# The attention output of a decoder trunk, split into upper and lower part per two head pairs instead of per four

## The chip, the cores and the metric

The kernel runs on one core of a Trainium2 chip. The metric is the device time of one execution in microseconds (us). Five engines take part, each with an instruction stream of its own that it runs in order: TensorE (PE in the profile; its weight loads are PEld), VectorE (DVE), ScalarE (ACT), GpSimd (POOL) and SyncE (SP), which issues most loads. They wait for one another by semaphores.

## The reference

A trunk of two layers on 256 tokens with 1024 channels, in float32. The first layer mixes tokens with a recurrent block, the second with forgetting attention over 16 heads of 64 channels. Each layer has a SwiGLU FFN ahead of and behind its mixer. The part that is changed is the attention:

```python
def forgetting_attention(xq, w_q, w_o, k, v, c):
    q = (xq @ w_q).reshape(Bn, S, N_HEADS, HEAD_DIM).transpose(0, 2, 1, 3) * (HEAD_DIM ** -0.5)
    for blk in range(S // Q_BLOCK):              # two blocks of 128 queries
        q0 = blk * Q_BLOCK; end = q0 + Q_BLOCK
        logits = einsum('bhqd,bhkd->bhqk', q[:, :, q0:end], k[:, :, :end])
        logits = logits + c[:, :, q0:end, None] - c[:, :, None, :end]
        logits = where(kpos <= qpos, logits, -inf)
        p = softmax(logits, axis=-1)
        outs.append(einsum('bhqk,bhkd->bhqd', p, v[:, :, :end]))
    o = concatenate(outs, axis=2).transpose(0, 2, 1, 3).reshape(Bn, S, D_ATTN)
    return o @ w_o
```

Its result goes through an RMS norm and is added to the residual stream; then comes the last FFN.

## The kernel before

**Numbers.** TensorE gets each float32 operand as two parts: an upper part, rounded to TensorE's fp32r type, and a lower part, the difference. A product is three matmuls: `mm3` gives upper by upper (L207), upper by lower of the weights (L208), and lower by upper (L209). Every weight is loaded into a tile `raw` and split by `split`: ScalarE copies it to `whi` (L199), VectorE subtracts to get `wlo` (L200). The attention output is split in the same way, into `oh` (L1206, ScalarE) and `ol` (L1207, VectorE).

**Tokens and work items.** The 256 tokens are two halves t of 128. Work comes as items, each with one weight tile of 128x1024. For each half there are eight items of the query projection and then eight of the output projection W_o. W_o's item k (`row_items`, L474) multiplies the k-th 128 rows of W_o, which belong to one pair of heads, by tile k of `oh` and `ol`; it takes six matmuls, three for each half of the 1024 columns. The last two items of a half are done together, column half by column half.

**The attention of one half** (`attention(t)`, L1143) goes by groups of heads: half 0 sees 128 keys and has four groups of two pairs, half 1 sees 256 keys and has eight groups of one pair. Each group passes through four parts:

- logits: matmuls of keys and queries (L1162) into two of the banks 4 to 7, bias (L1169) and maximum (L1171) on VectorE, exponentials with their sums (L1177) on ScalarE, reciprocal (L1179) and multiplication (L1180) on VectorE, into a tile `pe`;
- turn: four transposes of `pe` on TensorE (L1186) into a bank, copied out by ScalarE as `pT` (L1188);
- values: matmuls of `pT` with the values (L1200) into an accumulator `po`, one 128x128 block for each pair;
- the split of `po` into `oh` and `ol` (L1206, L1207), once its 512 columns are full, so for every four pairs.

Step i of a half does the values of group i-3, the turn of group i-2 and the logits of group i, in this order.

**What sets the order.** TensorE's stream is the order of the code, and that is set by a string, `ATT_ORDER`: "0" and "1" are the next item of half 0 or 1, "a0" and "a1" the next step of the attention of half 0 or 1. It runs from `0 0 0 0 0 0 0 a0 0 a0 1 1 1 a0 1 1 a0 1 1 a0 1 a1 0 a0` over alternating `a1 0` and `a1 1` to `1 1 1 1`. The streams of VectorE and ScalarE are put in order when the program is built, by a scheduler with times of its own; some parts have priority there, the residual update (`enter`) among them.

**The banks.** The accumulators, `po`, the transposes and the query tokens share banks 0 to 3 of PSUM, one tile `pall`:

```python
    def bank(kind, hold=False, again=False):

        free = [i for i in order[kind] if i not in held and i not in lent]
        i = free[-1 if again else 0]
        order[kind].remove(i)
        order[kind].append(i)
```

`mmbank()` takes the free bank that was asked for longest ago and holds it until `release`. The turn asks with `again=True` and gets the free bank that was asked for last. A bank may be written again when all that reads its old content has run, and matmuls wait for that. While half 0 is under way, W_o's accumulators and those of the query projection hold one or two of the four banks.

**Around the change**, W_o of half 0 begins after the fifth "a0" and W_o of half 1 after W_o of half 0, whose end starts its residual update on VectorE (L312, L316). `htok` (L1026) and `qT` (L1032) are the queries' tokens and their transposed copy. `nb` is the bias, `mx`, `sm` maximum and sum, `rstd` the norm's factor.

Of the kernel before, what the change touches and what calls it, by code (L numbers as in the profile page):

```python
# [9 lines left out]
F32 = mybir.dt.float32  # L10
F32R = mybir.dt.float32r
BF16 = mybir.dt.bfloat16
AF = mybir.ActivationFunctionType
ALU = mybir.AluOpType
AX = mybir.AxisListType

P = 128
D = 1024
S = 256
# [25 lines left out]
def trunk_kernel(ctx: ExitStack, tc: tile.TileContext, A: dict, out: bass.AP):  # L45
    nc = tc.nc
# [11 lines left out]
    def nm(s):  # L58
        uid[0] += 1
        return f"{s}_{uid[0]}"  # L60
# [6 lines left out]
# [6 lines that stand above are left out]
        b = pall[:, i, :]  # L73
        if hold:
            held[i] = b
        return b

    def release(*banks):
        for b in banks:
            for i in [i for i, v in held.items() if v is b]:  # L80
                del held[i]

    def mmbank():
        return bank("mm", True)
# [1040 lines left out]
    att = {}  # L1125
# [17 lines left out]
    def attention(t):  # L1143

        ap = pools["a"]
        nk = t + 1
        per = 4 // nk
        np_ = per // 2
        w = nk * P
        box = {}  # L1150
        G = NH // per

        def head(hg, b, j):
            return 2 * (hg * np_ + j) + b

        def logits(hg):
            c = 4 + (hg % 2) * 2
            lg = pall[:, c:c + 2, :S]
            for j in range(np_):
                for b in range(2):  # L1160
                    p = hg * np_ + j
                    nc.tensor.matmul(lg[:, b, j * w:(j + 1) * w], att["q"][t][b * HD:(b + 1) * HD, p, :],  # L1162
                                     kv["kT"][b * HD:(b + 1) * HD, p, :w], start=True, stop=True)
            v = lg.rearrange("p b (j k) -> p j b k", j=np_)
            h0 = hg * per
            bias = att["nb"][t][:, h0:h0 + per, :].rearrange("p (j b) k -> p j b k", b=2)
            if np_ == 1:
                v, bias = lg, att["nb"][t][:, h0:h0 + per, :]
            nc.vector.tensor_tensor(v, v, bias, ALU.add)  # L1169
            mx = spool.tile([P, 4], F32, tag="mx", name=nm("mx"))[:, :per]  # L1170
            nc.vector.tensor_reduce(mx, lg.rearrange("p b (j k) -> p b j k", j=np_), AX.X, ALU.max, negate=True)  # L1171
            sm = spool.tile([P, 4], F32, tag="sm", name=nm("sm"))[:, :per]
            pe = box["pe", hg] = ap.tile([P, per, w], F32, tag="pe", name=nm("pe"), bufs=2)
            for b in range(2):
                for j in range(np_):
                    i = b * np_ + j
                    nc.scalar.activation(pe[:, i, :], lg[:, b, j * w:(j + 1) * w], AF.Exp, bias=mx[:, i:i + 1],  # L1177
                                         accum_out=sm[:, i:i + 1])
            nc.vector.reciprocal(sm, sm)  # L1179
            nc.vector.tensor_tensor(pe, pe, sm.unsqueeze(2).to_broadcast([P, per, w]), ALU.mult)  # L1180

        def turn(hg):
            tp = bank("mm", again=True)
            pev = box["pe", hg].rearrange("p a b -> p (a b)")
            for j in range(4):
                nc.tensor.transpose(tp[:, j * P:(j + 1) * P], pev[:, j * P:(j + 1) * P], ident)  # L1186
            pT = box["pT", hg] = ap.tile([P, 4, P], F32, tag="pT", name=nm("pT"), bufs=2)
            nc.scalar.activation(pT.rearrange("p a b -> p (a b)"), tp, AF.Copy)  # L1188

        def values(hg):  # L1190
            p0 = hg * np_
            if p0 % 4 == 0:
                box["po"] = mmbank()
            po, pT = box["po"], box["pT", hg]
            for j in range(np_):
                o = (p0 + j) % 4 * P
                for k in range(nk):
                    for b in range(2):
                        hd = head(hg, b, j)
                        nc.tensor.matmul(po[b * HD:(b + 1) * HD, o:o + P], kv["v"][k][:, hd * HD:(hd + 1) * HD],  # L1200
                                         pT[:, (b * np_ + j) * nk + k, :], start=k == 0, stop=k == nk - 1)
            if (p0 + np_) % 4 == 0:
                b = (p0 + np_) // 4 - 1
                oh_v = att["oh"][t][:, 4 * b:4 * b + 4, :].rearrange("p a b -> p (a b)")
                ol_v = att["ol"][t][:, 4 * b:4 * b + 4, :].rearrange("p a b -> p (a b)")
                nc.scalar.activation(oh_v, po, AF.Copy)  # L1206
                nc.vector.tensor_tensor(ol_v, po, oh_v.bitcast(F32), ALU.subtract)  # L1207
                release(po)

        steps = []  # L1210
        for i in range(G + 3):
            s = []
            if 0 <= i - 3 < G:
                s.append(lambda i=i: values(i - 3))
            if 0 <= i - 2 < G:
                s.append(lambda i=i: turn(i - 2))
            if i < G:
                s.append(lambda i=i: logits(i))
            steps.append(s)
        return steps  # L1220
# [13 lines left out]
    ffn_d = ffn_items(lambda: pools["f"], A["ffn2_w_gate"][1], A["ffn2_w_up"][1], A["ffn2_w_down"][1], A["ffn2_post_g"][1],  # L1234
                      lambda t, hid: None, last=True)

    ATT_ORDER = ("0 0 0 0 0 0 0 a0 0 a0 1 1 1 a0 1 1 a0 1 1 a0 1 a1 0 a0 0 a1 0 a0 0 a1 0 a1 0 a1 0 a1 0 a1 1 a1 1 a1 1 a1 1 a1 1 1 1 1")


    def half(t, i):  # L1240
# [106 lines left out]
    nxt = [n_ffn3, n_ffn3]  # L1347
    for c in ATT_ORDER.split():
        if c[0] == "a":
# [45 lines left out]
```

## Time and profile before

| | us |
|---|---|
| median of 3 runs (1004.5 to 1004.77) | 1004.73 |
| the profiled execution | 1004.95 |
| its span, first to last instruction | 1003.2 |
| TensorE busy | 985.8 |
| VectorE busy | 676.1 |
| ScalarE busy | 562.1 |
| last W_o matmul of half 1 starts at | 810.14 |
| L1206, four copies of 128x512, each | 0.60 |
| L1207, four subtractions of 128x512, each | 0.68 |

In a row of the timeline stand the start, the duration, the engine, the line, the operation with output and inputs, the size, the count, and in brackets the idle time ahead of it on its engine with what ended that. A row with xN merges N instructions that follow each other. Matmuls overlap: one of 512 columns shows some 0.39 us, though the next starts 0.23 later. In a row of stretches stand from:to, length, and for PE, PEld, DVE, ACT and POOL the busy time and count, then the granted TensorE clock (1.00 is full), the DMA share and GB/s. In a row of groups stand line, engine, operation, sizes, count, then busy us and mean ns of one.

### The profile page before, as it was taken

To read this page: it belongs to the slowest core of one execution; us is meant where nothing else is said; L and a number is where in the kernel's file an instruction comes from. 1 tells how busy PE (TensorE), PEld (TensorE's weight loads), DVE (VectorE), ACT (ScalarE), POOL (GpSimd) and SP (SyncE) were. 2 spreads that over 40 slices of the span, in tenths; PEclk is the share of its full clock that TensorE was granted. 3 is DMA by queue.
4 is the path that set the end of the run, shared out by engine and by line. 5 is a ranking of instruction groups with operands and counts; after the bars stand their busy time and mean duration, and the time that the engine had idled before them with its cause. 6 is when DMAs were issued, how large, how long until landed. Compare 5 with 4: busy or idle time off the path is not lost.

```text
span 1003.2 us, 13846 instructions
## 1 busy us (share of the span) xinstructions
PE 985.8 (98%) x5272; PEld 831.9 (83%) x5272; DVE 676.1 (67%) x784; ACT 562.1 (56%) x732; POOL 50.8 (5%) x97
## 2 busy tenths in 40 slices
PE   8999999999999999999999999999999999999997
PEld 5888888789988888888898888888876678888886
DVE  5877664668998676664596676674588757666642
ACT  5656544559986555543565455553466656555431
POOL 1500000000003000000000000000030000000000
PEclk9999999999999999999999999999999999999999
DMA  6886655565427666545468666655485157665431
GB/s 231 275 272 200 199 164 189 156 184 151 137 81 248 214 188 186 189 158 186 114 204 277 190 181 196 199 188 160 156 294 168 43 151 248 188 191 187 153 123 42
DMA packets 94104, 182.06 MB, mean 181 GB/s; under 512 B 11838, under 2 KB 33430, under 8 KB 93910
## 3 DMA queue, kind: packets, MB, share of 16 engines
q1 hardware_dynamic: 92790, 180.06, 57.5%
q10 hardware_dynamic: 608, 1.06, 0.3%
q8 instruction: 41, 0.67, 0.3%
q0 software_dynamic: 640, 0.07, 0.1%
q14 instruction: 25, 0.20, 0.1%
HBM read 180.09 MB, written 1.06 MB: 181 GB/s over the span
## 4 chain that ended last, share of the span: by engine, by line
PE 68%; issue 22%; ACT 5%; DVE 4%; POOL 1%; DMA 0%; DVEq 0%; POOLq 0%; ACTq 0%
PE pall L232 23%; PE pall L233 12%; PE pall L207 9%; PE pall L209 9%; PE pall L208 9%; PE pall L858 1%; PE pall L214 1%; PE pall L215 1%; PE pall L216 1%; ACT junk L246 1%; DVE wlo L200 1%; ACT whi L199 1%; POOL rstd L241 1%; PE pall L255 1%; DVE h L316 1%
## 5 line engine op out<-in xcount | busy, mean ns | idle before, releaser
L200 DVE TENSOR_TENSOR wlo<-raw,whi 128x1024 fp32r<-128x1024 f32 (+4 forms) x329 | 395.0, 1207 | 249.5 <-ACT whi L199 246.8
L199 ACT ACTIVATE whi<-raw 128x1024 fp32r<-128x1024 f32 (+4 forms) x329 | 342.2, 1045 | 297.8 <-PE pall L209 119.1
L232 PE MATMUL pall<-xall,whi 128*128 128x512 f32 x1216 | 427.1, 397 | 0.0
L233 PE MATMUL pall<-xall,wlo 128*128 128x256 f32 x1216 | 339.6, 279 | 0.0
L232 PEld LDWEIGHTS pall<-xall,whi 128*128 128x128 f32 x1216 | 228.3, 188 | 55.2
L233 PEld LDWEIGHTS pall<-xall,wlo 128*128 128x128 f32 x1216 | 229.1, 188 | 0.1
L207 PE MATMUL pall<-whi,hid 128*128 128x512 f32 (+2 forms) x400 | 153.1, 383 | 0.5 <-ACT v L1109 0.5
L209 PE MATMUL pall<-whi,hid 128*128 128x512 f32 (+2 forms) x400 | 152.4, 381 | 0.0
L208 PE MATMUL pall<-wlo,hid 128*128 128x512 f32 (+2 forms) x400 | 152.3, 381 | 0.0
L207 PEld LDWEIGHTS pall<-whi,hid 128*128 128x128 f32 x400 | 75.1, 188 | 14.6 <-ACT v L1109 0.8
L208 PEld LDWEIGHTS pall<-wlo,hid 128*128 128x128 f32 x400 | 75.1, 188 | 13.6
L209 PEld LDWEIGHTS pall<-whi,hid 128*128 128x128 f32 x400 | 75.1, 188 | 13.7
L207 PE MATMUL pall<-whi,xall 128*128 128x512 f32 (+2 forms) x168 | 67.1, 399 | 0.4 <-DVE t L312 0.3
L208 PE MATMUL pall<-wlo,xall 128*128 128x512 f32 (+2 forms) x168 | 64.9, 386 | 0.4 <-DVE wlo L1258 0.2
L209 PE MATMUL pall<-whi,xall 128*128 128x512 f32 (+2 forms) x168 | 64.9, 386 | 0.1
L239 POOL TENSOR_SCALAR nv<-ss 128x1 f32<-128x1 f32 x24 | 10.2, 425 | 937.0 <-ACT junk L246 936.9
L208 PEld LDWEIGHTS pall<-wlo,xall 128*128 128x128 f32 x168 | 31.7, 188 | 7.5 <-DVE wlo L200 1.2
L209 PEld LDWEIGHTS pall<-whi,xall 128*128 128x128 f32 x168 | 31.5, 188 | 7.1 <-DVE xall L269 1.2
L207 PEld LDWEIGHTS pall<-whi,xall 128*128 128x128 f32 x168 | 31.6, 188 | 6.9 <-DVE t L312 0.7
L604 ACT ACTIVATE hid<-prod 128x1024 fp32r<-128x1024 f32 (+1 forms) x21 | 20.6, 981 | 23.0 <-DVE prod L600 23.0
L310 DVE SCALAR_TENSOR_TENSOR t<-pall,rstd,gb 128x512 f32<-128x512 f32 x16 | 11.9, 749 | 26.7 <-ACT junk L246 26.7
L594 ACT ACTIVATE sil<-sil 128x1024 f32<-128x1024 f32 (+1 forms) x21 | 20.6, 982 | 14.3 <-DVE sil L593 14.2
(192 smaller groups left out, 1007.9 us busy)
## 6 DMA issues: line engine op xcount, KB each, us to landing
raw<-in_ffn_w_down_dram SPq DMA_DIRECT2D x88, 512.0 KB
raw<-in_ffn_w_up_dram SPq DMA_DIRECT2D x80, 512.0 KB
raw<-in_ffn_w_gate_dram SPq DMA_DIRECT2D x79, 512.0 KB
raw<-in_rg_w_in_dram SPq DMA_DIRECT2D x20, 504.0 KB
raw<-in_rg_w_out_dram SPq DMA_DIRECT2D x10, 504.0 KB
raw<-in_ffn_w_gate_dram SPq DMA_DIRECT2D x18, 256.0 KB
raw<-in_ffn_w_up_dram SPq DMA_DIRECT2D x16, 256.0 KB
raw<-in_w_kv_dram SPq DMA_DIRECT2D x8, 512.0 KB
```

What stands on the lines that cost most here:

```text
L199: nc.scalar.activation(hi[:parts, c:c + m], rawv[:, c:c + m], AF.Copy)
L200: nc.vector.tensor_tensor(lo[:parts, c:c + m], rawv[:, c:c + m], hi[:parts, c:c + m].bitcast(F32), ALU.subtract)
L207: nc.tensor.matmul(ps, xh, wh, start=first, stop=False)
L208: nc.tensor.matmul(ps, xh, wl, start=False, stop=False)
L209: nc.tensor.matmul(ps, xl, wh, start=False, stop=last)
L214: nc.tensor.matmul(ps, wh, xh, start=first, stop=False)
L232: nc.tensor.matmul(o, wh, both, start=k == 0, stop=False)
L233: nc.tensor.matmul(oh, wl, upper, start=False, stop=k == 7)
L239: nc.gpsimd.tensor_scalar(v, ss[:, 0:1], ss[:, 1:2] if n == 2 else 0.0, D * EPS * f * f, ALU.add, ALU.add)
L310: nc.vector.scalar_tensor_tensor(t1[n], pf[n], r_in, gb[:, n * 512:(n + 1) * 512], ALU.mult, ALU.mult)
L594: nc.scalar.activation(s, s, AF.Silu)
L604: nc.scalar.activation(hv, pv, AF.Copy)
```

## The change

`po` is split whenever two pairs are in it, not four, so it uses only the first 256 columns of its bank. In half 0 each group now takes a bank for `po`, fills it, splits it and releases it; in half 1 that takes two groups. The copies and subtractions are eight instead of four, with 256 columns each. The string `ATT_ORDER` is only broken into two lines and has the same entries.

```diff
         def values(hg):
             p0 = hg * np_
-            if p0 % 4 == 0:
+            if p0 % 2 == 0:
                 box["po"] = mmbank()
             po, pT = box["po"], box["pT", hg]
             for j in range(np_):
-                o = (p0 + j) % 4 * P
+                o = (p0 + j) % 2 * P
...
-            if (p0 + np_) % 4 == 0:
-                b = (p0 + np_) // 4 - 1
-                oh_v = att["oh"][t][:, 4 * b:4 * b + 4, :].rearrange("p a b -> p (a b)")
-                ol_v = att["ol"][t][:, 4 * b:4 * b + 4, :].rearrange("p a b -> p (a b)")
-                nc.scalar.activation(oh_v, po, AF.Copy)
-                nc.vector.tensor_tensor(ol_v, po, oh_v.bitcast(F32), ALU.subtract)
+            if (p0 + np_) % 2 == 0:
+                k0 = p0 + np_ - 2
+                oh_v = att["oh"][t][:, k0:k0 + 2, :].rearrange("p a b -> p (a b)")
+                ol_v = att["ol"][t][:, k0:k0 + 2, :].rearrange("p a b -> p (a b)")
+                nc.scalar.activation(oh_v, po[:, :S], AF.Copy)
+                nc.vector.tensor_tensor(ol_v, po[:, :S], oh_v.bitcast(F32), ALU.subtract)
                 release(po)
```

TensorE's stream keeps its 4894 rows and their order. The banks differ: before, `po` of half 0 is in bank 3 and then bank 0, and the turns of groups 1, 2 and 3 write banks 0, 2 and 2. Now `po` of the four groups is in banks 3, 0, 2 and 2, and the turns of groups 1, 2 and 3 write banks 3, 0 and 2, each right behind the values of the group before; the first turn of half 1 writes bank 2. The built program lets the first transpose of each of these four turns wait for the L1207 subtraction of the bank it writes. In half 1 `po` is always in bank 0, and its next use waits for the last L1207.

VectorE's stream differs from the values of group 0 on. Before, from the weight subtraction that runs beside these values (numbers at the end of names count buffers; `pe_6645` and `sm_6644` belong to group 2 of half 0, `pe_6696` and `sm_6695` to group 3):

```order
L200 TENSOR_TENSOR wlo_6675<-raw_6672,whi_6674 128x1024
L1179 RECIPROCAL sm_6644<-sm_6644 128x4
L1169 TENSOR_TENSOR pall<-pall,nb_6455 128x2x2x128
L1180 TENSOR_TENSOR pe_6645<-pe_6645,sm_6644 128x512
L1171 TENSOR_REDUCE mx_6693<-pall 128x4
L200 TENSOR_TENSOR wlo_6717<-raw_6714,whi_6716 128x1024
L200 TENSOR_TENSOR wlo_6729<-raw_6726,whi_6728 128x1024
L1179 RECIPROCAL sm_6695<-sm_6695 128x4
L1026 TENSOR_SCALAR htok_6750<-pall,rstd_6511 128x512
L1180 TENSOR_TENSOR pe_6696<-pe_6696,sm_6695 128x512
L1207 TENSOR_TENSOR ol_6470<-pall,oh_6468 128x512
```

The same place on VectorE now (group 3 is `pe_6698`, `sm_6697`):

```order
L200 TENSOR_TENSOR wlo_6675<-raw_6672,whi_6674 128x1024
L1179 RECIPROCAL sm_6644<-sm_6644 128x4
L1207 TENSOR_TENSOR ol_6470<-pall,oh_6468 128x256
L1180 TENSOR_TENSOR pe_6645<-pe_6645,sm_6644 128x512
L1169 TENSOR_TENSOR pall<-pall,nb_6455 128x2x2x128
L1171 TENSOR_REDUCE mx_6695<-pall 128x4
L1179 RECIPROCAL sm_6697<-sm_6697 128x4
L1180 TENSOR_TENSOR pe_6698<-pe_6698,sm_6697 128x512
L200 TENSOR_TENSOR wlo_6719<-raw_6716,whi_6718 128x1024
L200 TENSOR_TENSOR wlo_6731<-raw_6728,whi_6730 128x1024
L1207 TENSOR_TENSOR ol_6470<-pall,oh_6468 128x256
```

The first subtraction stands right behind the reciprocal of group 2; the second behind the whole softmax of group 3, which has moved ahead of the two weight subtractions.

ScalarE's stream at the same place, before (`pT_6686` is the turn of group 1, `qT` a query tile):

```order
L199 ACTIVATE whi_6674<-raw_6672 128x1024
L1188 ACTIVATE pT_6686<-pall 128x512
L1177 ACTIVATE pe_6645,sm_6644<-pall,mx_6642 128x128 x4
L199 ACTIVATE whi_6716<-raw_6714 128x1024
L1032 ACTIVATE qT_6466<-pall 128x512
L199 ACTIVATE whi_6728<-raw_6726 128x1024
L1177 ACTIVATE pe_6696,sm_6695<-pall,mx_6693 128x128 x4
L1206 ACTIVATE oh_6468<-pall 128x512
```

And ScalarE's now:

```order
L199 ACTIVATE whi_6674<-raw_6672 128x1024
L1206 ACTIVATE oh_6468<-pall 128x256
L1177 ACTIVATE pe_6645,sm_6644<-pall,mx_6642 128x128 x4
L1188 ACTIVATE pT_6688<-pall 128x512
L1177 ACTIVATE pe_6698,sm_6697<-pall,mx_6695 128x128 x4
L1032 ACTIVATE qT_6466<-pall 128x512
L199 ACTIVATE whi_6718<-raw_6716 128x1024
L199 ACTIVATE whi_6730<-raw_6728 128x1024
L1206 ACTIVATE oh_6468<-pall 128x256
```

The first copy stands ahead of the exponentials of group 2, the copy of the transposes behind them; both weight copies stand behind the exponentials of group 3. The streams of GpSimd and SyncE keep their rows and order.

More of the change, by code (lines that the diff above doesn't have):

```diff
@@ L1235, in trunk_kernel @@
                       lambda t, hid: None, last=True)
-    ATT_ORDER = ("0 0 0 0 0 0 0 a0 0 a0 1 1 1 a0 1 1 a0 1 1 a0 1 a1 0 a0 0 a1 0 a0 0 a1 0 a1 0 a1 0 a1 0 a1 1 a1 1 a1 1 a1 1 a1 1 1 1 1")
+    ATT_ORDER = ("0 0 0 0 0 0 0 a0 0 a0 1 1 1 a0 1 1 a0 1 1 a0 1 a1 0 a0 0 a1 0 a0 0 a1 0 a1 0 a1 0 a1 0 a1 "
+                 "1 a1 1 a1 1 a1 1 a1 1 1 1 1")
     def half(t, i):
```

## The prediction

> **What bounds the kernel now.** I read the page's engine table first, then the busy time by stretches (from 745 us, just ahead of the attention's first exponentials, to 815, where the last FFN has begun, and from there to 1000), then the timeline of the attention.
>
> ```profile
> PE 985.8 (98%) x5272; PEld 831.9 (83%) x5272; DVE 676.1 (67%) x784; ACT 562.1 (56%) x732; POOL 50.8 (5%) x97
> ...
> 745.00:815.00 70.00, 65.14 (x388) 45.82 (x387) 55.76 (x83) 46.21 (x113) 5.32 (x8) 1.00 0.44 138
> 815.00:1000.00 185.00, 181.75 (x939) 154.44 (x937) 106.81 (x99) 86.54 (x95) 2.74 (x7) 1.00 0.50 158
> ```
>
> TensorE is busy 98% of the span: what its in-order stream loses or wins in the attention reaches the end nearly whole. In the first stretch it misses 4.9 us of 70, VectorE is at 80%, and the DMA share of 0.44 leaves room; after 815 TensorE hardly waits, so nothing later gives a delay back. The timeline shows what the change aims at, the waits of the first W_o matmuls for the two parts of the attention output:
>
> ```profile
> 764.95 0.47 PE L207 MATMUL pall<-whi,oh 128*128 128x512 f32 x1 [0.30 <-ACT pT L1188]
> 767.18 0.66 PE L1200 MATMUL pall<-pT,v 128*64 128x128 f32 x8
> 770.81 0.50 PE L207 MATMUL pall<-whi,oh 128*128 128x512 f32 x1
> 772.39 0.66 PE L1200 MATMUL pall<-pT,v 128*64 128x128 f32 x8
> ...
> 789.19 0.50 PE L207 MATMUL pall<-whi,oh 128*128 128x512 f32 x1
> 790.88 0.68 DVE L1207 TENSOR_TENSOR ol<-pall,oh 128x512 fp32r<-128x512 f32 x1
> 791.61 0.50 PE L209 MATMUL pall<-whi,ol 128*128 128x512 f32 x1 [1.69 <-DVE ol L1207]
> 792.74 0.66 PE L1200 MATMUL pall<-pT,v 128*64 128x128 f32 x8
> ...
> 802.13 0.66 PE L1200 MATMUL pall<-pT,v 128*64 128x128 f32 x8
> 803.84 0.50 PE L207 MATMUL pall<-whi,oh 128*128 128x512 f32 x1 [1.04 <-ACT oh L1206]
> 805.25 0.50 PE L209 MATMUL pall<-whi,ol 128*128 128x512 f32 x1 [0.68 <-DVE ol L1207]
> ```
>
> **What it removes.** Undisturbed, the six matmuls of a W_o item take 772.39 - 770.81 = 1.58 us. The first item of token half 0 takes 767.18 - 764.95 = 2.23; the first of half 1, 792.74 - 789.19 = 3.55. The later start at 803.84 comes 1.71 after the values matmuls, where 0.59 is usual (756.14 to 756.73, below), and its third matmul 1.41 after the first, where 2/6 of 1.58 = 0.53 is usual. In the change the two tiles that each of these items reads are split a group or two earlier, so all go: 0.65 + 1.97 + 1.12 + 0.88 = 4.62 us. At 792.74, though, the next values matmuls now open a new accumulator in bank 0, which they may write only when the lower part of the one before has been read from it. That subtraction stays behind the two residual updates and starts at 790.88; at half width it ends near 791.28, TensorE goes on at 791.33 where it would have been ready at 789.19 + 1.58 = 790.77: 0.56 comes back. Gain: 4.06.
>
> **What it adds on the other engines.** Four more copies and four more subtractions, each of half the width. Neither width stands here, so the nearest rows are taken:
>
> ```profile
> L295 ACT ACTIVATE rrow<-pall 128x256 f32<-128x256 f32 x5 | 1.9, 379 | 5.0 <-PE pall L293 5.0
> L936 DVE TENSOR_TENSOR y<-pall,tt 126x256 f32<-126x256 f32 x2 | 0.8, 404 | 0.0
> ```
>
> 0.38 and 0.40 us. Beside TensorE's 70 us that is hidden; it counts only where TensorE waits for it.
>
> **What it adds on TensorE: a wait in front of the transposes.** TensorE's own instructions and their order stay as they are. In token half 0 a group fills two tiles, so the accumulator is now taken and released within one step, and the transposes that follow ask for the free bank taken last: that very bank. Before, the accumulator was held over two groups, and they got another one. So three turns (transposes of groups 1, 2, 3) now wait until ScalarE and VectorE have both read the bank, and where the scheduler put these reads decides:
>
> ```profile
> 756.14 0.66 PE L1200 MATMUL pall<-pT,v 128*64 128x128 f32 x8
> 756.24 1.06 ACT L199 ACTIVATE whi<-raw 128x1024 fp32r<-128x1024 f32 x1 [0.29 <-PE pall L209]
> 756.73 0.66 PE L1186 MATMUL pall<-ident,pe 128*128 128x128 f32 x4
> 757.01 2.35 DVE L200 TENSOR_TENSOR wlo<-raw,whi 128x1024 fp32r<-128x1024 f32 x2
> 757.31 0.71 PE L1162 MATMUL pall<-kT,qT 64*128 64x128 f32 x8
> 759.44 0.18 DVE L1179 RECIPROCAL sm<-sm 128x4 f32<-128x4 f32 x1
> 759.54 0.67 DVE L1169 TENSOR_TENSOR pall<-pall,nb 128x512 f32<-128x512 f32 x1
> 761.96 0.66 PE L1186 MATMUL pall<-ident,pe 128*128 128x128 f32 x4
> ...
> 779.18 0.70 DVE L1169 TENSOR_TENSOR pall<-pall,nb 128x512 f32<-128x512 f32 x1
> 780.72 0.48 ACT L1177 ACTIVATE pe<-pall,mx 128x256 f32<-128x256 f32 x1 [1.61 <-DVE mx L1171]
> ...
> 762.44 0.35 ACT L1177 ACTIVATE pe<-pall,mx 128x128 f32<-128x128 f32 x1
> 763.72 0.21 ACT L1177 ACTIVATION_READ_ACCUMULATOR pe<-pall,mx 128x1 f32 x1
> ...
> L1032 ACT ACTIVATE qT<-pall 128x512 f32<-128x512 f32 x4 | 2.4, 601 | 2.0 <-PE pall L1031 2.0
> 751.75 2.05 ACT L199 ACTIVATE whi<-raw 128x1024 fp32r<-128x1024 f32 x2
> ```
>
> *Turn 1* (756.73). The subtraction now stands on VectorE behind two weight subtractions and a reciprocal. The former end at 757.01 + 2.35 = 759.36. The reciprocal needs four exponentials, ahead of which the copy now stands: 756.24 + 1.06 + 0.38, plus 1.49 for the four (762.44 to 763.93), gives 759.17, which is earlier. Reciprocal at 759.36, subtraction 0.10 later (759.44 to 759.54), end 759.86, and 0.05 to TensorE (790.88 + 0.68 = 791.56 to 791.61): 759.91. Cost 3.2 us.
>
> *Turn 2* (761.96, of its own 4.65 after the logits matmuls of 757.31, which move with turn 1). Its subtraction stands behind the whole softmax of those logits and two weight subtractions; ScalarE reaches the weights only after four exponentials and a query copy. From the logits' start: 0.71 + 0.05; bias and maximum until the exponentials 1.54 (779.18 to 780.72); four of them 1.49; copy 0.60; first weight copy 1.06; both weight subtractions 2.35; ours 0.40; 0.05. Sum 8.25, less about 0.2, since an instruction starts some 0.1 before the one ahead of it ends (two weight copies take 2.05, not 2.12): 8.05. Cost 8.05 - 4.65 = 3.4 us.
>
> *Turn 3*: here both reads follow at once: matmuls 0.66, copy 0.38, subtraction 0.40, three handovers of 0.05, less the usual 0.59: 1.0 us.
>
> ```profile
> 774.36 0.68 DVE L1207 TENSOR_TENSOR ol<-pall,oh 128x512 fp32r<-128x512 f32 x1
> 774.47 0.60 PE L1186 MATMUL pall<-ident,pe 128*128 128x128 f32 x4
> ...
> 781.97 0.69 DVE L1180 TENSOR_TENSOR pe<-pe,sm 128x512 f32<-128x512 f32 x1
> 782.62 0.66 PE L1200 MATMUL pall<-pT,v 128*64 128x128 f32 x8
> ...
> 795.74 0.68 DVE L1180 TENSOR_TENSOR pe<-pe,sm 128x512 f32<-128x512 f32 x1
> 796.73 0.66 PE L1186 MATMUL pall<-ident,pe 128*128 128x128 f32 x4
> ```
>
> *Three small ones in half 1.* Its first turn (774.47) reuses that bank too; the subtraction, now 0.40, ends at 774.76: 0.35. The values matmuls of 782.62 wait for a subtraction that stands behind the multiplication of 781.97: 782.66 + 0.40 + 0.05, cost 0.45. The turn at 796.73 needs a multiplication that ends 0.31 before it (796.42); TensorE comes 1.41 earlier there (1.97 - 0.56), so nothing is lost if that chain moves along and 1.10 if it doesn't; part of it does (the weight copy ahead of it need not wait so long), and I take 0.45.
>
> The order on SP's and GpSimd's queues stays; the weight loads behind the delayed subtractions come later together with the matmuls that need them. I cost that at nothing: the cover is the room in the DMA share and TensorE's own delay; without it a late weight would cost about its copy and subtraction, 1.06 + 1.18.
>
> **The sum.** Costs 3.2 + 3.4 + 1.0 + 0.35 + 0.45 + 0.45 = 8.85, gain 4.06, net +4.8 us. The profiled execution took 1004.95 (span 1003.2 and 1.75 around it), 0.22 over the median of 1004.73; on the median the forecast is 1009.5.
>
> **Rivals.**
>
> *The clock falls in the new gaps* (slower still). TensorE stands idle about 3.1 us before turn 1 and 3.3 before turn 2, longer than anywhere in the trace but its end:
>
> ```profile
> 1.51 3.60 PE L151 MATMUL pall<-idle 128*128 128x512 bf16 x8 [1.51 <-DVE idle L137]
> ...
> 996.37 0.39 PE L209 MATMUL pall<-whi,hid 128*128 128x512 f32 x1
> ...
> 999.50:999.75 0.25, 0.00 (x0) 0.00 (x0) 0.25 (x1) 0.00 (x0) 0.00 (x0) 0.52 0.00 0
> ```
>
> There the last matmul ends at 996.76, and the granted clock is at 0.52 from about 999.5, after 2.75 us. By that, both gaps can bring it down. At the start, not yet warm, eight 512-column matmuls take 3.60 us, 0.45 each; 1.58 / 6 = 0.26 is usual. Were it slow for about as long as it was idle, some 3.2 us, that loses 3.2 x (1 - 0.26/0.45) = 1.35 for each gap: 1010.9 for one, 1012.2 for both. Against it: the 1.69 us wait at 791.61 left the clock at 1.00. The Trainium skill (TensorE: Matmul & The Clock Gate, Part 1: The HAM clock gate) says that the clock halves after at least one idle window of some 3.4 us that runs on its own phase; by that rule neither gap holds a whole window and the sum stays 1009.5, but the fall after 2.75 us in this trace doesn't agree with a full window of idleness.
>
> *The reads follow at once.* If VectorE were free when the upper copy ends, turns 1 and 2 would cost what turn 3 does: net 3 x 1.0 + 1.25 - 4.06 = +0.2, 1004.9, no change. For it: turn 3. Against it: VectorE runs its instructions in the built order, and in both places long ones stand ahead.
>
> *Only the gain* (faster). If the turns did not meet the accumulator's bank, costs in turns 1 to 3 and in 774.47 fall away: 0.9 - 4.06 = -3.2, 1001.5. It decides whether the subtraction ends before 756.73 and 761.96. Since the copy can't start before the matmuls that end at 756.80, that needs another bank, which the rule of the bank list speaks against.
>
> **How the numbers follow.** Forecast case 0.58, clock 0.26, reads at once 0.08, only the gain 0.04, something slower than 1012.2 (late weights) 0.04. A measurement tells this kernel from no change at about 0.2%, 2 us: faster 0.04, same 0.08, slower 0.88. The range runs from 1007.1, where VectorE gets to the subtraction one weight subtraction (1.18) earlier in both turn 1 and turn 2, to 1012.2, both clock falls.
>
> **What would show it.** In the trace of the changed kernel: the L1186 transposes of groups 1 and 2 in half 0 idle over 3 us each on the lower subtraction, group 3 about 1; the waits of W_o's third matmuls for that subtraction gone; from 756 to 771 a delay that grows to about 6.5 us and comes down to about 4.8 by 815, where it stays. A clock under 1.00 near 760 or 768 shows the first rival. I am wrong if the first transposes after the values start at their usual 0.59, or if TensorE catches up after 815.

## The result, and the profile after

| | before | after |
|---|---|---|
| median, us | 1004.93 | 1010.5 |
| lowest to highest of six executions | 1004.5 to 1008.37 | 1009.72 to 1011.86 |
| the profiled execution | 1004.95 | 1009.83 |
| its span | 1003.2 | 1008.1 |

The change makes the kernel slower: the ratio is 1.0049, with a 95% interval of 1.0038 to 1.0059. The six executions after lie in two clusters, 1009.72 to 1009.83 and 1011.16 to 1011.86; the profiled one is of the lower.

The page's engine line of the kernel after, and the stretches that answer to those of before:

```profile
PE 985.9 (98%) x5272; PEld 833.1 (83%) x5272; DVE 676.4 (67%) x788; ACT 562.1 (56%) x736; POOL 52.7 (5%) x97
...
745.00:815.00 70.00, 61.43 (x368) 43.49 (x367) 51.39 (x81) 43.75 (x113) 5.02 (x6) 0.98 0.36 115
815.00:1000.00 185.00, 184.71 (x952) 156.92 (x952) 108.57 (x102) 88.56 (x97) 3.20 (x7) 1.00 0.50 165
```

TensorE has as many instructions as before and is busy as long. In the attention it stands still 8.6 us of 70, where it was 4.9, and the granted clock of that stretch is 0.98. What TensorE waits for from 745 to 825, in the view of the waits (engine, line, what released it: us in total, times, longest):

```profile
PE pall L1186 <- DVE ol L1207: 6.5, 4, 3.0
PE pall L1200 <- DVE ol L1207: 1.3, 2, 0.6
```

The waits of W_o's third matmuls (L209) for the lower part are gone. In their place four turns (L1186) and two values matmuls (L1200) wait for the lower part's reading of a bank. The timeline gives each in its place; first four rows of before that the prediction did not show, then TensorE after:

```profile
761.37 0.66 PE L1200 MATMUL pall<-pT,v 128*64 128x128 f32 x8
767.77 0.66 PE L1186 MATMUL pall<-ident,pe 128*128 128x128 f32 x4
787.38 0.66 PE L1200 MATMUL pall<-pT,v 128*64 128x128 f32 x8
810.83 0.50 PE L207 MATMUL pall<-whi,xall 128*128 128x512 f32 x1 [0.30 <-DVE t L312]
```

```profile
755.87 0.66 PE L1200 MATMUL pall<-pT,v 128*64 128x128 f32 x8
759.54 0.73 PE L1186 MATMUL pall<-ident,pe 128*128 128x128 f32 x4 [3.01 <-DVE ol L1207]
765.70 0.66 PE L1200 MATMUL pall<-pT,v 128*64 128x128 f32 x8
768.76 0.66 PE L1186 MATMUL pall<-ident,pe 128*128 128x128 f32 x4 [2.41 <-DVE ol L1207]
773.23 0.66 PE L1200 MATMUL pall<-pT,v 128*64 128x128 f32 x8
774.83 0.66 PE L1186 MATMUL pall<-ident,pe 128*128 128x128 f32 x4 [0.94 <-DVE ol L1207]
...
781.88 0.66 PE L1186 MATMUL pall<-ident,pe 128*128 128x128 f32 x4 [0.17 <-DVE ol L1207]
...
790.59 0.66 PE L1200 MATMUL pall<-pT,v 128*64 128x128 f32 x8 [0.65 <-DVE ol L1207]
...
795.35 0.66 PE L1200 MATMUL pall<-pT,v 128*64 128x128 f32 x8
...
799.42 0.66 PE L1200 MATMUL pall<-pT,v 128*64 128x128 f32 x8 [0.61 <-DVE ol L1207]
...
803.73 0.66 PE L1186 MATMUL pall<-ident,pe 128*128 128x128 f32 x4 [0.25 <-DVE pe L1180]
...
809.13 0.66 PE L1200 MATMUL pall<-pT,v 128*64 128x128 f32 x8
...
815.74 0.50 PE L207 MATMUL pall<-whi,xall 128*128 128x512 f32 x1 [0.29 <-DVE t L312]
```

The profiled execution after is 756.14 - 755.87 = 0.27 us ahead when the changed part begins. Counted from there, the delay at each place is the start after, less the start before, plus 0.27:

| place (start before, after) | delay | added here | predicted |
|---|---|---|---|
| turn 1 (756.73, 759.54) | 3.08 | +3.08 | +3.2 |
| values of group 1 (761.37, 765.70) | 4.60 | +1.52 | 0 |
| turn 2 (761.96, 768.76) | 7.07 | +2.47 | +3.4 |
| values of group 2 (767.18, 773.23) | 6.32 | -0.75 | -0.65 |
| turn 3 (767.77, 774.83) | 7.33 | +1.01 | +1.0 |
| first turn of half 1 (774.47, 781.88) | 7.68 | +0.35 | +0.35 |
| values (782.62, 790.59) | 8.24 | +0.56 | +0.45 |
| values (787.38, 795.35; then 792.74, 799.42) | 8.24, 6.95 | -1.29 | -1.97 + 0.56 |
| turn (796.73, 803.73) | 7.27 | +0.32 | +0.45 |
| first matmul behind W_o (810.83, 815.74) | 5.18 | -2.09 | -1.12 - 0.88 |

5.18 less the 0.27 is 4.91, and the spans differ by 4.9: all of it comes from the attention. One line was not in the forecast's sum, the 1.52 us between turn 1 and the values of group 1, where TensorE waits for nothing. The view of stretches shows what it is:

```profile
759.50:760.00 0.50, 0.46 (x4) 0.42 (x4) 0.50 (x1) 0.00 (x0) 0.00 (x0) 1.00 0.73 180
760.00:760.50 0.50, 0.50 (x4) 0.30 (x4) 0.09 (x1) 0.19 (x1) 0.00 (x0) 0.50 1.03 401
...
763.00:763.50 0.50, 0.50 (x3) 0.40 (x2) 0.00 (x0) 0.46 (x3) 0.00 (x0) 0.58 0.02 8
763.50:764.00 0.50, 0.50 (x4) 0.37 (x4) 0.00 (x0) 0.50 (x4) 0.00 (x0) 1.00 0.00 0
```

From 760.0 to some 763.4 the granted clock is 0.50; the fall comes half a microsecond after TensorE has come back from its first gap. After the second gap, which ends at 768.76, it stays at 1.00 in this execution.

Who makes turns 1 and 2 wait can be read on VectorE and ScalarE:

```profile
756.74 2.35 DVE L200 TENSOR_TENSOR wlo<-raw,whi 128x1024 fp32r<-128x1024 f32 x2
756.94 0.36 ACT L1206 ACTIVATE oh<-pall 128x256 fp32r<-128x256 f32 x1
...
759.10 0.39 DVE L1207 TENSOR_TENSOR ol<-pall,oh 128x256 fp32r<-128x256 f32 x1
...
766.01 2.36 DVE L200 TENSOR_TENSOR wlo<-raw,whi 128x1024 fp32r<-128x1024 f32 x2 [0.53 <-ACT whi L199]
766.81 0.39 ACT L1206 ACTIVATE oh<-pall 128x256 fp32r<-128x256 f32 x1
768.29 0.42 DVE L1207 TENSOR_TENSOR ol<-pall,oh 128x256 fp32r<-128x256 f32 x1
```

Each time the copy is through early (757.30, 767.20), and the subtraction, 0.4 us of work, stands behind two weight subtractions. At turn 2 these have themselves waited, 0.53 us, for ScalarE's weight copies.

### The profile page after: what moved, and what is told of

Same layout as the page of the kernel before. It is cut to its first block, busy times and chain, and to the rows that moved or that the text cites. A ratio compares the mean times of both kernels' runs of the same rounds, so it can differ in the third digit from the quotient of the medians.

```text
span 1008.1 us, 13854 instructions
## 1 busy us (share of the span) xinstructions
PE 985.9 (98%) x5272; PEld 833.1 (83%) x5272; DVE 676.4 (67%) x788; ACT 562.1 (56%) x736; POOL 52.7 (5%) x97
## 4 chain that ended last, share of the span: by engine, by line
PE 66%; issue 22%; DVE 5%; ACT 5%; POOL 1%; DMA 0%; DVEq 0%; ACTq 0%; POOLq 0%
PE pall L232 23%; PE pall L233 11%; PE pall L207 9%; PE pall L209 9%; PE pall L208 9%; DVE wlo L200 1%; PE pall L858 1%; PE pall L214 1%; PE pall L215 1%; PE pall L216 1%; ACT whi L199 1%; ACT junk L246 1%; ACT pe L1177 1%; POOL rstd L241 1%; PE pall L255 1%
## 5 line engine op out<-in xcount | busy, mean ns | idle before, releaser
L209 PE MATMUL pall<-whi,hid 128*128 128x512 f32 (+2 forms) x400 | 152.5, 381 | 0.0
L209 PEld LDWEIGHTS pall<-whi,hid 128*128 128x128 f32 x400 | 75.1, 188 | 13.8
L209 PE MATMUL pall<-whi,xall 128*128 128x512 f32 (+2 forms) x168 | 65.1, 388 | 0.1
L209 PEld LDWEIGHTS pall<-whi,xall 128*128 128x128 f32 x168 | 31.8, 189 | 7.1 <-DVE xall L269 1.1
```

The lines of the kernel that those rows point to most:

```text
L209: nc.tensor.matmul(ps, xl, wh, start=False, stop=last)
```

## The experiments

The theory has three parts. The loss is the wait for a bank that has just been read. Its size is VectorE's queue. The gaps that it leaves lower the clock, which also spreads the executions. The rivals are that the additional instructions themselves cost the time, that the gain is not there, and that the spread has another cause. Each kernel was timed beside runs of the kernel before; the ratio compares those executions and is not the quotient of the two medians.

| kernel | median (lowest to highest), us | before beside it | ratio (95%) |
|---|---|---|---|
| e1, bank released later | 1001.6 (1001.16 to 1002.28) | 1006.39 | 0.9957 (0.9946 to 0.9969) |
| e7, turns take another bank | 1002.58 (1002.23 to 1003.37) | 1005.83 | 0.9963 (0.9950 to 0.9976) |
| e3, half 1 alone | 1002.43 (1002.04 to 1003.04) | 1006.39 | 0.9966 (0.9954 to 0.9978) |
| e4, half 0 alone | 1013.3 (1012.63 to 1015.84) | 1006.39 | 1.0079 (1.0066 to 1.0093) |
| e5, before with halved instructions | 1007.8 (1005.91 to 1009.43) | 1006.39 | 1.0018 (1.0009 to 1.0028) |
| e2, reads given priority | 1005.95 (1005.1 to 1006.79) | 1005.28 | 1.0002 (0.9993 to 1.0011) |
| e6, both gaps filled | 1009.06 (1008.86 to 1009.48) | 1005.28 | 1.0037 (1.0025 to 1.0050) |
| e8, gap 1 filled | 1010.76 (1010.16 to 1011.21) | 1005.83 | 1.0044 (1.0029 to 1.0058) |
| e9, gap 2 filled | 1010.37 (1009.87 to 1010.46) | 1005.83 | 1.0038 (1.0024 to 1.0053) |
| e10, before with its waits filled | 1004.84 (1004.42 to 1005.39) | 1005.83 | 0.9990 (0.9981 to 0.9999) |
| e12, e1 and e2 together | 1001.27 (1000.82 to 1001.81) | 1005.28 | 0.9960 (0.9946 to 0.9973) |

**Is it the bank? (e1, e7)** Two ways to keep the turn off the bank just read. In e1 `po` is given back one step later:

```diff
             if p0 % 2 == 0:
+                old = box.get("po")
                 box["po"] = mmbank()
+                if old is not None:
+                    release(old)
...
-                release(po)
+                if p0 + np_ == 8:
+                    release(po)
```

> The split per two head pairs as in the change, but an accumulator's bank is given back only when the next accumulator has been taken, so that the transposes that follow get another bank and need not wait for the two reads of it. Theory (the cost is the wait for the bank): the waits of the transposes of groups 1 and 2 of half 0 for the lower part go (3.1 and 2.5 us in the changed kernel), group 3's falls to under 1, the clock stays at 1.00 all through 756 to 775, and only the gain and the small costs of half 1 are left: 4.06 less 0.9 to 1.5, so 2.5 to 3.2 us faster than before, 1001.5 to 1002.5. Rival (the additional copies and subtractions themselves, or their place on ScalarE and VectorE, cost the time): slower than before, 1005 to 1010.

In e7 the turn asks differently:

```diff
-            tp = bank("mm", again=True)
+            tp = bank("mm", again=t == 1)
```

> The change with one word altered: in half 0 the transposes ask for the free bank that was asked for longest ago, not for the one asked for last. Theory (the cost is that the transposes meet the bank just read): in half 0 they take another bank than the accumulator, which stays in one bank; nothing but the values matmuls of the next group waits for the lower part, and that is ready by then; the gaps are gone, the clock stays up, and the time is that of the later release, 3 to 3.5 us faster than before, 1001.3 to 1002. Rival (any order in which half 0 has its parts split per two pairs waits, since VectorE reaches the subtraction late): the wait moves to the values matmuls or to the query transposes, 1004 to 1007.

Both are faster than before and than the change. TensorE of e1 in the timeline, and its stretch from 755 to 775:

```profile
756.06 0.66 PE L1203 MATMUL pall<-pT,v 128*64 128x128 f32 x8
756.65 0.66 PE L1186 MATMUL pall<-ident,pe 128*128 128x128 f32 x4
...
761.29 0.66 PE L1203 MATMUL pall<-pT,v 128*64 128x128 f32 x8
761.88 0.66 PE L1186 MATMUL pall<-ident,pe 128*128 128x128 f32 x4
```

```profile
755.00:775.00 20.00, 19.59 (x123) 13.60 (x122) 16.57 (x28) 13.87 (x39) 0.00 (x0) 1.00 0.60 193
```

Turns 1 and 2 follow their values after the usual 0.59, the clock is 1.00, and the copies and subtractions are as many and as wide as in the change. So they are not the loss; the bank is. The span falls by 1003.2 - 999.9 = 3.3. In e7 the gain is a little less, 1002.58 where 1001.3 to 1002 was expected, and the profile names a new wait:

```profile
PE pall L1200 <- DVE htok L1026: 1.0, 1, 1.0
```

With the turns elsewhere, a values matmul meets the bank from which the query tokens are read. The rival of e7, a moved wait, is right by this one microsecond and not by more.

**Where do gain and loss lie? (e3, e4)** The number of pairs is set for each half:

```diff
+        pm = 4 if t == 0 else 2
...
-            if p0 % 2 == 0:
+            if p0 % pm == 0:
...
-            if (p0 + np_) % 2 == 0:
-                k0 = p0 + np_ - 2
+            if (p0 + np_) % pm == 0:
+                k0 = p0 + np_ - pm
```

e4 has `2 if t == 0 else 4`; the widths of copy and subtraction follow `pm`.

> Only half 1 is split per two pairs; half 0 is split per four pairs as before. Theory (gain and cost lie in different halves): the gain at the first W_o item of half 1 and at 803.84, less its small costs: 1.97 + 1.12 + 0.88 - 0.56 - 0.45 - 0.45 = 2.5 us faster than before, about 1002.4. Rival (an earlier split gains nothing, since the delay returns at the next wait): 1004.3 to 1005.2.

> Only half 0 is split per two pairs; half 1 is split per four pairs as before. Theory: the three waits of the transposes in half 0, with the changed kernel's measured sizes 3.1 + 2.5 + 1.0, the loss of about 1.5 at a lowered clock between 760 and 765, less the gain of 0.65 at the first W_o item: 7.4 us slower than before, about 1012.3, and some executions 1.3 to 1.5 above or below that, by whether the clock falls. The difference of this run and that of the split in half 1 alone add to that of the change, about 5. Rival (part of the delay is taken up by half 1's own waits): 1008 to 1010.

Half 1 alone has a span of 1000.8, 2.4 less than before, as expected. Half 0 alone has 1011.0, 7.8 more, where 7.4 was expected; its executions reach from 1012.63 to 1015.84, so the expected 1012.3 was low. The two differences add to 5.4; the change has 4.9. (In e4's trace the values of group 0 start at 756.18, 0.31 later than in that of the change, so a part of this lies ahead of the attention.) The whole gain but the 0.75 of the first W_o item is in half 1, and the loss is in half 0.

**Do the instructions cost anything? (e5)** The kernel before, with its copy and its subtraction cut in two:

```diff
-                nc.scalar.activation(oh_v, po, AF.Copy)
-                nc.vector.tensor_tensor(ol_v, po, oh_v.bitcast(F32), ALU.subtract)
+                for c in range(2):
...
+                    nc.scalar.activation(oh_v, po[:, c * S:c * S + S], AF.Copy)
+                    nc.vector.tensor_tensor(ol_v, po[:, c * S:c * S + S], oh_v.bitcast(F32), ALU.subtract)
```

> The kernel before with its copy and its subtraction each written as two instructions of half the width at the same place: the number of instructions of the change without its time and without its banks. Theory (hidden beside TensorE): within 0.2% of before, 1004 to 1006; the subtraction of group 7's accumulator ends perhaps 0.1 later. Rival (four more instructions on ScalarE and VectorE each cost what they take): 3 us slower.

Neither expectation is quite met: it is 0.18% slower, just inside the bound, with its median above the 1004 to 1006 expected (the kernel before had 1006.39 beside it), and the span has 1.0 us more. It isn't the sum of their durations, which the rival put at 3 us. Its executions spread over 3.5 us with a mean granted clock of 0.995 to 0.999, and how much of the 0.18% is the clock is not shown. The trace at the first W_o item of half 0:

```profile
765.33 1.23 DVE L200 TENSOR_TENSOR wlo<-raw,whi 128x1024 fp32r<-128x1024 f32 x1
...
766.48 0.42 DVE L1209 TENSOR_TENSOR ol<-pall,oh 128x256 fp32r<-128x256 f32 x1
...
766.95 0.50 PE L207 MATMUL pall<-whi,oh 128*128 128x512 f32 x1 [1.00 <-DVE ol L1209]
```

The second subtraction stands behind a weight subtraction, and the W_o accumulator of the upper 512 columns waits for its bank. Cutting an instruction in two lets others in between.

**Is it VectorE's queue? (e2, e12)** The change, with priority for the two reads; e12 adds the later release of e1:

```diff
+                with tc.high_priority():
...
```

> The change with the copy and the subtraction of the attention output given priority in the scheduler: on VectorE they move ahead of one weight subtraction in groups 1 and 2, with the banks as in the change. Theory (what stands ahead on VectorE sets the wait, and the clock falls in a gap over about 2.7 us only): the transposes of groups 1 and 2 wait about 1.2 us less each than in the changed kernel, 2 and 1.3 us, the clock stays at 1.00, 2.4 + 1.5 us less in all: 1006 to 1007.5, with executions close together. Rival (the wait is set by the weight copies or the softmax and not by the weight subtractions): as the changed kernel, 1009.7 to 1011.5.

> Both: the later release of the bank and the priority of the copy and the subtraction. Theory: the transposes of half 0 have no wait for the bank, and in half 1 the values matmuls and the turns wait less for the lower part: 3.2 to 4.1 us faster than before, 1000.7 to 1001.6. Rival (priority delays a weight subtraction or a softmax that TensorE then waits for): 0.5 to 1.2 worse than with the later release alone.

In e2 one weight subtraction less stands ahead, and the turns wait less. TensorE in the timeline, then its stretches:

```profile
758.36 0.66 PE L1186 MATMUL pall<-ident,pe 128*128 128x128 f32 x4 [1.83 <-DVE ol L1208]
...
766.19 0.66 PE L1186 MATMUL pall<-ident,pe 128*128 128x128 f32 x4 [0.94 <-DVE ol L1208]
```

```profile
759.50:760.00 0.50, 0.50 (x6) 0.36 (x3) 0.47 (x2) 0.15 (x1) 0.00 (x0) 1.00 0.72 193
760.00:760.50 0.50, 0.50 (x3) 0.41 (x2) 0.50 (x2) 0.00 (x0) 0.00 (x0) 0.71 0.99 369
...
763.00:763.50 0.50, 0.50 (x2) 0.35 (x2) 0.34 (x1) 0.50 (x4) 0.00 (x0) 0.50 0.48 184
763.50:764.00 0.50, 0.50 (x3) 0.41 (x2) 0.50 (x1) 0.50 (x4) 0.00 (x0) 0.88 0.05 16
```

The waits fell from 3.01 to 1.83 and from 2.41 to 0.94, and the median is 4.5 us below that of the change: VectorE's queue sets them. The 0.94 is what turn 3 shows in the change, where the reads follow at once. But the clock went down here too, for about 3.4 us, after a gap of only 1.83. The theory had said that it takes 2.7; that part falls. e12 has none of these waits left (the longest of TensorE from 745 to 825 is 0.54 us, for the query tokens), and e1's time.

**Is the rest the clock? (e6, e8, e9, e10)** Twelve matmuls ahead of the turns of groups 1 and 2 (e6), of group 1 (e8) or of group 2 (e9):

```diff
         def turn(hg):
+            if t == 0 and hg in (1, 2):
+                for _ in range(FILL):
+                    nc.tensor.matmul(pall[:, 8 - 2 * hg, :P], ident, ident, start=True, stop=True)
```

> The change with twelve matmuls of the identity with itself ahead of the transposes of groups 1 and 2 of half 0, into banks that are free there; nothing reads them. They fill the gaps that the wait for the bank leaves. Theory (the spread of the changed kernel's executions, 1009.7 to 1011.9, is the clock that falls once or twice in the gaps): clock 1.00 in all windows from 756 to 775, the eight logits matmuls after the transposes of group 1 and the third W_o or weight matmuls at their usual duration, executions within 0.5 us of each other, at 1008.2 to 1009.5. Rival (the spread comes from elsewhere): the same spread and the same median as the changed kernel.

> The change with twelve matmuls of the identity with itself in the gap ahead of the transposes of group 1 only; nothing reads them. Theory (each gap of its own can lower the clock for some 3.3 us, and a loss in the second gap is given back by nothing): executions at about 1009.1 where the clock holds and at 1010.6 to 1010.8 where it falls, so a spread of about 1.6. Rival (only the first gap lowers it): all within 0.5 us of 1009.1.

> The same, in the gap ahead of the transposes of group 2 only. Theory (the first gap lowers the clock, and some 0.9 of the 1.5 us that this costs shortens the wait of group 2, whose end VectorE and ScalarE set): all executions at 1009.1 to 1009.9, none from 1010.5 up. Rival (the upper cluster of the changed kernel comes from the first gap): two clusters 1.5 to 2 us apart.

In e6 the executions lie within 0.62 us of each other, where the change has 2.14; the clock is 1.00 from 755 to 775. TensorE in the timeline, the fillers ahead of the turn each time (fillers are L1186 there, each in two rows; the turn is L1190):

```profile
755.80 0.66 PE L1204 MATMUL pall<-pT,v 128*64 128x128 f32 x8
756.39 2.94 PE L1186 MATMUL pall<-ident 128*128 128x128 f32 x24
759.47 0.66 PE L1190 MATMUL pall<-ident,pe 128*128 128x128 f32 x4
...
764.72 2.94 PE L1186 MATMUL pall<-ident 128*128 128x128 f32 x24
767.96 0.66 PE L1190 MATMUL pall<-ident,pe 128*128 128x128 f32 x4 [0.29 <-DVE ol L1211]
...
772.43 0.66 PE L1204 MATMUL pall<-pT,v 128*64 128x128 f32 x8
```

So with the clock held, turn 1 is late by 759.47 - 756.39 = 3.08 and turn 2 by 767.96 - 764.72 = 3.24. (VectorE's order differs a little there: one of the two weight subtractions stands ahead of the reciprocal of group 3.) From the values of group 0 to those of group 2 it takes 772.43 - 755.80 = 16.63 us; the change takes 773.23 - 755.87 = 17.36. So the fall after gap 1 costs 0.73 in all.

In e8, whose second gap is open, the six executions lie at 1010.16 to 1011.21, their median 1.7 above that of e6; none is at 1009.1, so the expected second cluster is missing. Its profile shows the fall while TensorE still waits, and the clock back within 771 to 772; the values of groups 0 and 2 stand below it:

```profile
767.00:768.00 1.00, 0.00 (x0) 0.00 (x0) 1.00 (x2) 0.01 (x1) 0.00 (x0) 0.90 0.92 352
768.00:771.00 3.00, 2.62 (x8) 2.24 (x9) 0.33 (x1) 0.60 (x1) 0.00 (x0) 0.50 0.71 200
```

```profile
756.23 0.66 PE L1204 MATMUL pall<-pT,v 128*64 128x128 f32 x8
...
774.16 0.66 PE L1204 MATMUL pall<-pT,v 128*64 128x128 f32 x8
```

That is 17.93, so the fall after gap 2 costs 17.93 - 16.63 = 1.30. The rest of the 1.7 is not the fall: 0.43 lies ahead of the attention, which begins at 756.23 here and at 755.80 in e6. Single executions differ there by some tenths.

In e9, whose first gap is open, the clock falls after it (0.50 from 760.9 to 764.3 in its profile) and no execution is above 1010.46. The median is 1.3 above e6 and not the 0 to 0.8 expected. The fillers of 2.94 us outlast what the fall leaves of the second wait:

```profile
766.54 2.94 PE L1186 MATMUL pall<-ident 128*128 128x128 f32 x24
769.32 0.60 PE L1190 MATMUL pall<-ident,pe 128*128 128x128 f32 x4
```

Turn 2 is late by 2.78, where the change has 2.47, so the fillers cost 0.31 beside the 0.73 of the fall; e9's attention also begins 0.28 later than e6's. By the profiles, then, the lower cluster of the change is one fall, after gap 1 (1009.06 + 0.73 = 1009.8). Two falls would make 1009.8 + 1.3 = 1011.1, the lower edge of the upper cluster, 1011.16 to 1011.86. That the upper executions had two was not seen in a trace of their own; their mean granted clock over the whole execution, 0.994 to 0.996, is below the 0.997 of the three lower ones and the 0.999 of e6.

The kernel before has two clusters as well. Beside these experiments it ran 49 times, 21 times at 1004.3 to 1005.28 and 28 times at 1005.58 to 1008.54. In e10 its waits at 791.61 and 803.84 are filled:

```diff
         nc.tensor.matmul(ps, xh, wl, start=False, stop=False)
+        for _ in range(fill):
+            nc.tensor.matmul(pall[:, 6, :P], ident, ident, start=True, stop=True)
         nc.tensor.matmul(ps, xl, wh, start=False, stop=last)
...
+                    if fill and (t, kk, n) == (1, 4, 0):
+                        for _ in range(fill // 2):
+                            nc.tensor.matmul(pall[:, 6, :P], ident, ident, start=True, stop=True)
```

> The kernel before with seven matmuls of the identity with itself in the wait of 1.69 us ahead of the third W_o matmul of half 1, and three in the wait of 1.04 us ahead of the W_o matmul at 803.84; nothing reads them. Theory (the executions of the kernel before lie at 1004.3 to 1005 and at 1006.4 to 1007.7 because the clock falls in these waits in a part of them): one cluster at 1004.3 to 1005, and against the changed kernel with its gaps filled (1009.1) the change without its clock costs 4.3 to 4.8. Rival (the spread comes from elsewhere): two clusters as before.

All twelve executions lie at 1004.42 to 1005.39, so the upper cluster is gone with the two waits. That they make it by the clock is not shown: there is no trace of an upper execution. The mean granted clock is 0.998 or 0.999 in all 21 lower executions; it is 0.994 or 0.996 in 15 of the 28 upper ones, but 0.998 or 0.999 in the other 13. Such a mean does not rule a fall out (e4's profiled execution has 0.998 and a fall in its trace), nor does it show one. With filled gaps on both sides the change costs 1009.06 - 1004.84 = 4.2, from two sets of runs; 4.3 to 4.8 was expected.

## Why the prediction was right

1010.5 was measured, 1009.5 forecast, with 1007.1 to 1012.2 as its range and 0.88 for slower. Slower is right, for the reason given: the transposes wait for the bank that has just been read, behind VectorE's queue. But the case that the forecast stands for, a clock that holds, is not what the trace of the change shows.

- **The gain, 4.06.** It measured 0.75 + 1.29 + 2.09 = 4.13. The rival "only the gain", 1001.5, is what e1 does once the turns have another bank: 1001.6. So it was rightly made to hang on the bank list.
- **Turn 1, 3.2, and turn 3, 1.0.** They measured 3.08 and 1.01, with the instructions ahead that the prediction named. "The reads follow at once" held for turn 3 alone.
- **Turn 2, 3.4.** It measured 2.47 in the change and 3.24 in e6. The working was right for a clock that holds: from the start of the logits matmuls to the turn it gave 8.05, and e6 took 767.96 - 760.05 = 7.91. With the fall, TensorE arrives 1.52 late, and the copies and subtractions that end the wait move less: 2.47 instead of 3.24, so some 0.8 of the loss is taken back. The prediction added clock and waits as if neither touched the other.
- **The three small ones, 1.25.** They measured 0.35 + 0.56 + 0.32 = 1.23.
- **The clock** is the step that failed. The forecast case held it at 1.00, at a chance of 0.58, and the fall was the rival at 0.26. In the profile of the change it fell, after gap 1 alone. The size of a fall, 1.35, was near: 1.52 after gap 1 in the change, of which 0.73 is left by the values of group 2, and 1.30 after gap 2 in e8. Its price came from an unsure place, though: at the start of the execution the stretches show the granted clock at 1.00 (1.5 to 5 us), so the 0.45 us of those matmuls is not shown to be a lowered clock. In the fall of the change, matmuls of 512 columns start 0.43 us apart (762.80 to 763.23).
- **The evidence on the clock.** Two pieces of it were read wrongly. "The 1.69 us wait at 791.61 left the clock at 1.00" was one execution; e10 shows that the upper cluster of the kernel before goes when this wait and the next one are filled. And the fall after 2.75 us at the end of the span had already spoken against the need for a longer gap; e2's came after 1.83. The Trainium skill (TensorE: Matmul & The Clock Gate, Part 1: The HAM clock gate) has the clock halve after at least one idle window of some 3.4 us. With that, e2's fall does not agree. The same section of the Trainium skill has the clock back at full after at least one busy window of some 3.4 us. The time that it stays down agrees with that length, about 3.4 us in the change, in e2 and in e8, though in e8 the first 0.6 us of it were idle.
- **The forecast came close** because its sum without falls, 1009.5, is near e6's 1009.06, and the falls add little: the two clusters lie some 0.7 and 2.4 above e6. With the clock held, the measured terms make 3.08 + 3.24 + 1.01 + 1.23 - 4.13 = 4.43, where 4.8 was forecast; turn 2 (0.16) and turn 1 (0.12) make most of the difference. The delay was to grow to 6.5 by 771 (the prediction's own terms make 3.2 + 3.4 - 0.65 + 1.0 = 6.95) and come down to 4.8 by 815; it was 7.33 at turn 3 and came down to 5.2. No wait for a late weight appeared, as costed.

## What to carry to other kernels

When a buffer is given back earlier, look at who takes it next: a rule that hands out the buffer used last turns two short reads into a wait for everything that stands ahead of them on the engines that read. Here the same split with the bank held one step longer is 0.4% faster than the kernel before (e1, e12), 0.3% faster than e10, where that kernel's waits are filled, and some 0.9% faster than the change. And price a gap of TensorE like these (1.83 to 3.16 us) with the clock that may fall in it, from several executions: one profile at 1.00 doesn't show that it holds.

## What was not expected of the hardware

- The granted clock went to half after idle times of TensorE of 1.83 us (e2), 3.01 (the change) and 3.16 (e8), and stayed there about 3.4 us each time, however long the gap was. It set in 3.5 us after TensorE stopped in the change (756.5 to 760.0), when work was under way again, and some 2.6 us after in e8 (765.2 to 767.8), when it was not. The length of the gap alone does not decide: gap 2 of the change, 2.41 us, was spared in the profiled execution, and the shorter one of e2 was not. Why, stays open.
- The kernel before, whose longest waits in the attention are 1.69 and 1.04 us, had 28 of 49 executions above its fastest cluster, by up to some 3.5 us; filling these two waits with matmuls of no use took that away without making the kernel slower. Whether the clock is the reason is not shown.
